# Up products of two FFNs as seven products of 2x2 blocks, weights in pieces, attention transposes moved: a kernel on one Trainium2 core

## The chip, the core and the metric

The kernel runs on one core of a Trainium2 chip. The core's engines work from their own queues: TensorE (PE) multiplies, VectorE (DVE), ScalarE (ACT) and GpSimd (POOL) work on elements, SyncE (SP) issues most of the transfers. The metric is the device time of one execution in microseconds; the figure for a kernel is the median of its runs.

## The reference, cut to what matters

Three blocks are computed on 512 tokens of width 1024, with a context of 256 tokens: two blocks of one kind (attention, pooling and convolution, then an FFN), which the text calls layers 0 and 1, and one of another kind (latent attention and a recurrence, then an FFN), layer 2. All is float32. The change bears on the FFN of layers 1 and 2, where only the 512 tokens are left:

```python
def swiglu(h, w_in, w_out):
    gu = jnp.einsum('bld,de->ble', h, w_in)
    g, u = jnp.split(gu, 2, axis=-1)
    return jnp.einsum('blf,fd->bld', jax.nn.silu(g) * u, w_out)

x = x + g1 * jnp.einsum('blm,md->bld', mix, w_out[l])
x = x + g2 * swiglu(modulate(rms_norm(x, norm2_g[l]), sh2, sc2), w_ffn_in[l], w_ffn_out[l])
```

with 2816 hidden columns. The vectors g1, g2, sh2, sc2 come from a modulation product of a condition vector with a weight w_mod.

## The kernel before, in words

**Products.** A float32 operand is held as two parts, hi (a rounded copy, made by ACT) and lo (the rest, a subtraction on POOL or DVE). `mm3` (L254, L257, L258) makes one product of 128 rows from three matmuls: hi x hi, hi x lo, lo x hi. Activations lie with features on the partitions: `h[k]` is a pair (hh, hl) of 128 features by 512 tokens, k from 0 to 7, and the tokens are worked on in two halves of 256.

**Weights.** The class `Weights` walks a list of all weights in the order of their use, one ahead. A weight of 2048 columns is fetched by SP in two transfers of 512 KB (tiles `raw`, four buffers), and split in four quarters of 512 columns: ACT's cast (L229, `whi`) and POOL's subtraction (L230, `wlo`). The pool `w` has two buffers of 2048 columns for each part.

**The FFN** (`ffn`) runs over 22 slices of 128 hidden columns. For each slice `j` the gate and the up product are each eight `mm3` over k, with 512 tokens as columns (in the first two slices as two times 256, so that the first half's products can run while the second half's norm is made). Then ACT's Silu (L948) and DVE's multiply (L949) read PSUM, ACT and POOL split the result (`gh`, `gl`), and `mod_fill` may put a slot of modulation products (L343) behind it. After a group of slices (the table `DOWN`: 8, 8, 2, 4 in layers 1 and 2) the down products of the group run and DVE adds them into x (`flush`, L888).

**Before the FFN** `out_proj` makes the output projection for one half of the tokens, then for the other; behind each the callback `norms` makes the half's row scale (`row_rms`, whose transposes are L322) and its normalized rows (`norm_apply`: L422, L430 on DVE; L425, L427 on ACT; L428 on POOL).

**Attention** (`attn`, `attn_values`; in layer 2 `mla_values`) goes over heads and blocks of 128 queries: scores of a block, then the values of the block before; with the second block of a pair, right behind its values, DVE's scaling (L862) and PE's two transposes (L865; L1542 in layer 2).

A scheduler puts the instructions of each engine in an order by priorities and estimated costs; each engine then works strictly through its own.

## Time and profile before

| | us |
|---|---|
| median of 3 runs | 2644.15 (2641.61 to 2648.14) |
| the profiled execution | 2645.27 |
| its span | 2643.4 |
| PE busy in it | 2505.2 (95%) |
| POOL, DVE, ACT busy | 1143.5, 959.3, 908.4 |
| mean granted clock of PE | 0.972 |

The profile's span has stages of two kinds: mixing (0 to 420, 1060 to 1400 and 1760 to 2260 us, about) and the FFNs of the layers 0, 1 and 2 between and behind them. PE's shares differ between them, so the share of the whole span says little about one. Durations of DVE and POOL are those between an instruction's start and its end, whatever it waited for inside.

### The profile page before, as it was taken

The numbers are of one execution on the slowest core, as the hardware profiler recorded it, in microseconds if no ns is written. First come the engines' busy times: TensorE is split into PE (matmuls) and PEld (weight loads), VectorE is DVE, ScalarE is ACT, GpSimd is POOL, SyncE is SP. The second block draws the span as 40 slices with busy tenths as digits, with TensorE's granted clock in tenths as the row PEclk, the third lists the DMA queues.
The fourth block names the chain that finished last, engine by engine and source line by source line (L and its number), as shares of the span: only waits on it lengthen the run. The fifth ranks groups of instructions, "written<-read, shape, count | busy, mean of one in ns | idle before, by whom it ended". The sixth has DMA issues, their size and how long they took to land.

```text
span 2643.4 us, 38643 instructions
## 1 busy us (share of the span) xinstructions
PE 2505.2 (95%) x15840; PEld 2134.2 (81%) x15840; DVE 959.3 (36%) x1932; ACT 908.4 (34%) x1905; POOL 1143.5 (43%) x965
## 2 busy tenths in 40 slices
PE   7889979999999999989999999999998899999998
PEld 5778869988888889877788777778887788888887
DVE  4897464221120123488542112113322756210112
ACT  4334443312212123333534223224443543422222
POOL 4544314523333334655326545454322344555553
PEclk9889989999999999999999999999998899999999
DMA  7113311323223222222224434343101021222221
GB/s 252 50 49 112 116 68 33 119 89 112 96 91 103 95 97 99 81 64 81 96 80 144 158 129 160 124 151 106 51 33 50 16 95 50 80 96 96 94 90 57
DMA packets 68961, 248.55 MB, mean 94 GB/s; under 512 B 7472, under 2 KB 10800, under 8 KB 67120
## 3 DMA queue, kind: packets, MB, share of 16 engines
q1 hardware_dynamic: 64992, 231.11, 26.8%
q10 hardware_dynamic: 3792, 14.97, 1.5%
q8 instruction: 125, 2.05, 0.3%
q14 instruction: 52, 0.43, 0.1%
HBM read 239.75 MB, written 6.29 MB: 93 GB/s over the span
## 4 chain that ended last, share of the span: by engine, by line
PE 47%; DVE 6%; ACT 2%; POOL 2%; issue 1%; DMA 1%; POOLq 0%; DVEq 0%; ACTq 0%
PE s2t L254 6%; PE s2t L258 6%; PE s2t L257 6%; PE pj L254 5%; PE pj L257 5%; PE pj L258 5%; PE ap L819 2%; DVE mix L664 1%; PE ap L254 1%; PE ap L257 1%; PE ap L258 1%; POOL wlo L230 1%; PE s2t L1525 1%; PE ap L343 1%; PE s2t L836 1%
## 5 line engine op out<-in xcount | busy, mean ns | idle before, releaser
L230 POOL TENSOR_TENSOR wlo<-raw,whi 128x512 fp32r<-128x512 f32 x576 | 747.2, 1328 | 713.5 <-ACT whi L229 710.3
L229 ACT CAST whi<-raw 128x512 fp32r<-128x512 f32 x576 | 319.7, 616 | 673.3 <-PE pj L257 243.6
L254 PE MATMUL s2t<-hh,whi 128*128 128x512 f32 (+1 forms) x1184 | 448.5, 380 | 1.0 <-ACT whi L229 1.0
L258 PE MATMUL s2t<-hh,wlo 128*128 128x512 f32 (+1 forms) x1184 | 446.7, 377 | 0.0
L257 PE MATMUL s2t<-hl,whi 128*128 128x512 f32 (+1 forms) x1184 | 445.8, 377 | 0.9 <-POOL hl L428 0.9
L254 PE MATMUL pj<-hh,whi 128*128 128x256 f32 (+1 forms) x1088 | 337.6, 312 | 8.0 <-ACT hh L425 2.7
L257 PE MATMUL pj<-hl,whi 128*128 128x256 f32 (+1 forms) x1088 | 332.5, 306 | 3.1 <-POOL hl L428 1.1
L258 PE MATMUL pj<-hh,wlo 128*128 128x256 f32 (+1 forms) x1088 | 331.3, 305 | 0.3 <-POOL wlo L230 0.3
L949 DVE TENSOR_TENSOR sg<-sg,s2t 128x512 f32<-128x512 f32 x66 | 45.4, 687 | 656.5 <-ACT sg L948 656.5
L258 PEld LDWEIGHTS s2t<-hh,wlo 128*128 128x128 f32 x1184 | 222.7, 188 | 46.6 <-issue 1.2
L254 PEld LDWEIGHTS s2t<-hh,whi 128*128 128x128 f32 x1184 | 222.3, 188 | 46.4 <-issue 2.1
L257 PEld LDWEIGHTS s2t<-hl,whi 128*128 128x128 f32 x1184 | 222.5, 188 | 45.8 <-POOL hl L428 1.5
L254 PEld LDWEIGHTS pj<-hh,whi 128*128 128x128 f32 x1088 | 210.6, 194 | 25.5 <-issue 3.7
L327 POOL TENSOR_TENSOR gl<-sg,gh 128x512 fp32r<-128x512 f32 (+1 forms) x66 | 97.5, 1477 | 299.8 <-ACT gh L326 299.8
L257 PEld LDWEIGHTS pj<-hl,whi 128*128 128x128 f32 x1088 | 211.2, 194 | 12.0 <-POOL hl L428 1.4
L258 PEld LDWEIGHTS pj<-hh,wlo 128*128 128x128 f32 x1088 | 210.2, 193 | 8.7 <-POOL wlo L230 0.5
L254 PE MATMUL pj<-whi,hh 128*128 128x256 f32 x672 | 196.8, 293 | 1.3 <-ACT v L699 0.9
L257 PE MATMUL pj<-wlo,hh 128*128 128x256 f32 x672 | 194.6, 290 | 0.0
L258 PE MATMUL pj<-whi,hl 128*128 128x256 f32 x672 | 194.0, 289 | 0.0
L888 DVE SCALAR_TENSOR_TENSOR xt<-pj,mod,xt 128x256 f32<-128x256 f32 x224 | 101.6, 480 | 177.1 <-PE pj L258 176.5
L948 ACT ACTIVATE sg<-s2t 128x512 f32<-128x512 f32 x66 | 39.2, 594 | 314.5 <-PE s2t L258 314.4
L254 PE MATMUL pj<-gh,whi 128*128 128x512 f32 (+1 forms) x400 | 145.6, 367 | 0.0
(382 smaller groups left out, 4581.6 us busy)
## 6 DMA issues: line engine op xcount, KB each, us to landing
raw<-in_w_mod SPq DMA_DIRECT2D x144, 512.0 KB, 3.9
raw<-in_w_up SPq DMA_DIRECT2D x132, 512.0 KB, 3.9
raw<-in_w_dn SPq DMA_DIRECT2D x66, 512.0 KB, 4.0
raw<-in_w_in SPq DMA_DIRECT2D x60, 512.0 KB, 3.9
raw<-in_w_out SPq DMA_DIRECT2D x24, 512.0 KB, 3.8
xt<-xs ACTq DMA_DIRECT2D x4, 1024.0 KB, 5.7
xt<-in_xT ACTq DMA_DIRECT2D x2, 1024.0 KB, 7.8
xs<-xt SPq DMA_DIRECT2D x2, 1024.0 KB, 3.8
```

Of the source, the lines that this page charges most:

```text
L229: nc.scalar.copy(out=h, in_=raw[:, q])
L230: nc.gpsimd.tensor_tensor(out=lo[:, s][:, q], in0=raw[:, q], in1=h.bitcast(F32), op=ALU.subtract)
L254: i = mm(ps, lhsT=lh, rhs=rh, start=start, stop=False)
L257: mm(ps, lhsT=lh, rhs=rl, start=False, stop=False)
L258: return mm(ps, lhsT=ll, rhs=rh, start=False, stop=stop)
L327: (lo_eng or self.nc.vector).tensor_tensor(out=lo, in0=src, in1=hi.bitcast(F32), op=ALU.subtract)
L343: nc.tensor.matmul(ps[g:g + 32], lhsT=self.cond_t[:, k, :], rhs=raw[k // 4][:, k % 4, :], start=k < 4, stop=k >= 4, tile_position=(0, g))
L664: nc.vector.scalar_tensor_tensor(out=m, in0=u[:, j:j + W], scalar=dw(j), in1=m, op0=ALU.mult, op1=ALU.add)
L819: i = nc.tensor.matmul(o, lhsT=at[:, j], rhs=v[:, j0 + j, :], start=j0 + j == 0, stop=j0 + j == nj - 1)
L888: self.nc.vector.scalar_tensor_tensor(out=x, in0=ps, scalar=col, in1=x, op0=ALU.mult, op1=ALU.add)
L948: nc.scalar.activation(out=sg[:, c], in_=p[:, 0], func=AF.Silu)
L949: nc.vector.tensor_tensor(out=sg[:, c], in0=sg[:, c], in1=p[:, 1], op=ALU.mult)
```

## The change

In layers 1 and 2 the gate and up products of one slice are seen as one product of 2x2 blocks: rows are gate (a1x) and up (a2x), the inner dimension is cut into k 0 to 3 and 4 to 7, the tokens into their two halves, b11 to b22. Instead of the eight block products the kernel makes seven, each of 4 k x 3 matmuls with 256 columns, out of sums of blocks: t1 to t4 of the activations (once for each layer) and s1 to s4 of the weights (once for each slice), and seven sums of the results.

- `norms_seven` makes b11 and b21 from the first half of the tokens, and from the second half, for each pair of k, two scaled rows, four differences and five splits (b12 itself is not needed: t1 stands in its place, and t2, t3, b22, t4 follow).
- `_load7` turns a slice's weight into seven pieces of 128x512, in six steps, one behind each product: four sums on DVE (L253, L254, L257, L262), four residues on DVE (L235), three on POOL, seven casts on ACT.
- `up_seven` makes the products, seven sums on DVE from PSUM (L995), and Silu, multiply (L1014, L1017) and split as before.
- All weights lie in pieces of 512 columns (pool `w` has eight buffers for each part), read through `View`.
- `DOWN` of layers 1 and 2 becomes that of layer 0: groups of 4, 4, 4, 4, 2, 4 slices. `MODS_FFN` of layer 1 puts three slots into each of its first two slices, and as many (22) in all.
- `attn_values` and `mla_values` return their transposes as a function `turn`, which the loop calls behind the next scores.

```diff
-DOWN = [
-    [(0, 4, 512), (4, 4, 512), (8, 4, 512), (12, 4, 512), (16, 2, 1024), (18, 4, 512)],
-    [(0, 8, 256), (8, 8, 256), (16, 2, 1024), (18, 4, 512)],
-    [(0, 8, 256), (8, 8, 256), (16, 2, 1024), (18, 4, 512)],
-]
+DOWN = [[(0, 4, 512), (4, 4, 512), (8, 4, 512), (12, 4, 512), (16, 2, 1024), (18, 4, 512)]] * 3
+SEVEN = (1, 2)
...
+    def _split(self, src, lo_eng, pool=None, bufs=None):
+        nc = self.k.nc
+        hi, lo = [(pool or self.k.p_w).tile([128, 512], F32R, tag=t, name=t, bufs=bufs) for t in ("whi", "wlo")]
+        nc.scalar.copy(out=hi, in_=src)
+        lo_eng.tensor_tensor(out=lo, in0=src, in1=hi.bitcast(F32), op=ALU.subtract)
+        return hi, lo
...
+        def first():
+            d["a11"] = self._split(a11, nc.gpsimd)
+            d["t1"], d["t2"] = [k.tmp("sq", [128, 512]) for _ in range(2)]
+            tt(out=d["t1"], in0=a21, in1=a22, op=ALU.add)
+            tt(out=d["t2"], in0=d["t1"], in1=a11, op=ALU.subtract)
+
+        def s3():
+            tt(out=a21, in0=a11, in1=a21, op=ALU.subtract)
+            d["s3"] = self._split(a21, v)
+
+        def s4():
+            d["a12"] = self._split(a12, nc.gpsimd, self.extra, 2)
+            tt(out=a12, in0=a12, in1=d["t2"], op=ALU.subtract)
+            d["s4"] = self._split(a12, v)
...
+        self.todo += [
+            first, lambda: part("s2", lambda: d["t2"], v), s3, lambda: part("s1", lambda: d["t1"], v), s4,
+            lambda: part("a22", lambda: a22, nc.gpsimd, self.extra, 2)]
...
+        p = product(x[:, 0], "a11", "b11")
+        nc.scalar.copy(out=r1, in_=p)
+        p = product(x[:, 1], "s2", "t2")
+        add(u2, r1, p)
+        p = product(y[:, 0], "s3", "t3")
+        add(u3, u2, p)
+        p = product(y[:, 1], "s1", "t1")
+        add(c22, u3, p)
+        add(u2, u2, p)
+        sg = pf.tile([128, 2, 256], F32, tag="sg", name="sg", bufs=2)
+        p = product(self.ps([128, 256]), "s4", "b22")
+        add(u2, u2, p)
+        nc.scalar.activation(out=sg[:, 1], in_=u2, func=AF.Silu)
+        p = product(self.ps([128, 256]), "a12", "b21")
+        add(r1, r1, p)
+        nc.scalar.activation(out=sg[:, 0], in_=r1, func=AF.Silu)
+        nc.vector.tensor_tensor(out=sg[:, 1], in0=sg[:, 1], in1=c22, op=ALU.mult)
+        p = product(self.ps([128, 256]), "a22", "t4")
+        add(u3, u3, p)
+        nc.vector.tensor_tensor(out=sg[:, 0], in0=sg[:, 0], in1=u3, op=ALU.mult)
...
+            for k in range(4):
+                x = value(1, k, r, self.scratch())
+                y = value(1, k + 4, r, self.scratch())
+                p, q = f1[k], f1[k + 4]
+                e, o = (nc.vector, nc.gpsimd)[::1 if k % 2 else -1]
+                sub(nc.vector, p, x, p)
+                self.split(*b["t1"][k], p, e)
+                sub(nc.vector, x, y, x)
+                self.split(*b["b22"][k], y, o)
+                sub(nc.vector, y, y, p)
+                self.split(*b["t2"][k], y, nc.vector)
+                self.split(*b["t3"][k], x, nc.gpsimd)
+                sub(nc.vector, q, q, y)
+                self.split(*b["t4"][k], q, e)
...
-    MODS_FFN = [[1] * NJ, [1] * NJ, [0] * NJ]
+    MODS_FFN = [[1] * NJ, [3, 3] + [1] * 14 + [0] * 2 + [1, 1, 0, 0], [0] * NJ]
...
                     with self.tc.high_priority(300):
                         e, nk = self.attn_scores(pa, l, hd, g, i, qk[hd], og)
-                        if prev is not None:
-                            self.attn_values(*prev)
+                        if turn is not None:
+                            turn()
+                        turn = self.attn_values(*prev) if prev is not None else None
...
-        self.p_w = es.enter_context(tc.tile_pool(name="w", bufs=2))
+        self.p_w = es.enter_context(tc.tile_pool(name="w", bufs=8))
```

Where the instructions come to stand, at three places. In the changed kernel `mm3` is L317, L320, L321; the row scale's transposes are L385; the residue of an activation split is L390.

**First, the start of layer 2's FFN.** On PE before, around the second half's row scale (`rsy`), `s2t` being the tiles of the first half's gate and up products:

```order
L254 MATMUL s2t<-hh,whi 128x256
L257 MATMUL s2t<-hl,whi 128x256
L258 MATMUL s2t<-hh,wlo 128x256
L254 MATMUL s2t<-hh,whi 128x256
L322 MATMUL ap<-ident,rsy 128x128 x2
L257 MATMUL s2t<-hl,whi 128x256
L258 MATMUL s2t<-hh,wlo 128x256
```

On PE after, 13 rows behind the same transposes (`pj` are the products with b21 and b22, `th` and `tl` the two parts of t1 to t4):

```order
L320 MATMUL pj<-hl,whi 128x256
L321 MATMUL pj<-hh,wlo 128x256
L317 MATMUL pj<-hh,whi 128x256
L320 MATMUL pj<-hl,whi 128x256
L321 MATMUL pj<-hh,wlo 128x256
L317 MATMUL s2t<-th,whi 128x256 x2
L320 MATMUL s2t<-tl,whi 128x256
L321 MATMUL s2t<-th,wlo 128x256
L317 MATMUL s2t<-th,whi 128x256
L320 MATMUL s2t<-tl,whi 128x256
L321 MATMUL s2t<-th,wlo 128x256
L317 MATMUL s2t<-th,whi 128x256
```

What moved: before, matmuls with `hh`, `hl` of the first half stand on both sides of the transposes. After, one product (`s2t<-hh`) stands ahead of them and products with b21 and b22 behind them, and the operands `th`, `tl`, of the second half, follow 18 rows on. On DVE before, from the second half's first scaling to the multiplies of the first slices:

```order
L422 SCALAR_TENSOR_TENSOR u<-xt_19628,mod_88,ap 128x256 x4
L430 SCALAR_TENSOR_TENSOR hl<-u,mod_88,hh 128x256
L422 SCALAR_TENSOR_TENSOR u<-xt_19628,mod_88,ap 128x256 x2
L430 SCALAR_TENSOR_TENSOR hl<-u,mod_88,hh 128x256
L422 SCALAR_TENSOR_TENSOR u<-xt_19628,mod_88,ap 128x256 x2
L430 SCALAR_TENSOR_TENSOR hl<-u,mod_88,hh 128x256 x2
L949 TENSOR_TENSOR sg<-sg,s2t 128x512 x8
```

and on DVE after, from the same scaling on:

```order
L1041 SCALAR_TENSOR_TENSOR u<-xt_21828,mod_88,ap 128x256 x4
L235 TENSOR_TENSOR wlo<-sq,whi 128x512
L1054 TENSOR_TENSOR f_22789<-u,f_22789 128x256 x2
L390 TENSOR_TENSOR hl<-u,hh 128x256
L253 TENSOR_TENSOR sq<-raw 128x512
L1054 TENSOR_TENSOR u<-u 128x256 x2
L390 TENSOR_TENSOR hl<-f_22789,hh 128x256
L257 TENSOR_TENSOR raw<-raw 128x512
L1054 TENSOR_TENSOR u<-u,f_22789 128x256 x2
L1054 TENSOR_TENSOR f_22807<-f_22807,u 128x256 x2
L262 TENSOR_TENSOR raw<-raw,sq 128x512
L390 TENSOR_TENSOR tl<-u,th 128x256 x2
```

What moved: the residues of the norm (L430) give way to differences (L1054), residues (L390) and weight steps (L235, L253, L257, L262) in one row; the whole stretch up to the first sum L995 is 30 rows of order.

**Second, a slice in layer 2's FFN.** On DVE a slice before is one row L949 (above, x8 for a group). After, in the first group:

```order
L995 TENSOR_TENSOR nm<-nm,s2t 128x256
L257 TENSOR_TENSOR raw<-raw 128x512
L995 TENSOR_TENSOR rt<-nm,s2t 128x256
L995 TENSOR_TENSOR nm<-nm,pj 128x256
L995 TENSOR_TENSOR rt<-rt,s2t 128x256
L995 TENSOR_TENSOR nm<-nm,s2t 128x256
L262 TENSOR_TENSOR raw<-raw,sq 128x512
L995 TENSOR_TENSOR nm<-nm,pj 128x256
L254 TENSOR_TENSOR sq<-sq,raw 128x512
L235 TENSOR_TENSOR wlo<-raw,whi 128x512
L995 TENSOR_TENSOR rt<-rt,pj 128x256
L1014 TENSOR_TENSOR sg<-sg,rt 128x256
```

What moved: seven sums (L995) and two multiplies stand among the sums and residues of the next slices' weights, in one queue.

**Third, PE in layer 0's attention** at the transposes L865 (L927 after) of the `on` tile that PE waits for at 339.67 us in the trace. Before:

```order
L258 MATMUL pj<-whi,hl 128x256
L791 MATMUL pj<-ident,y 128x128 x4
L819 MATMUL ap<-v,at 128x128 x3
L836 MATMUL s2t<-qk 128x512 x2
L865 MATMUL ap<-ident,on 128x128 x2
```

After:

```order
L896 MATMUL s2t<-qk 128x256 x6
L851 MATMUL pj<-ident,y 128x128 x4
L879 MATMUL ap<-v,at 128x128 x3
L896 MATMUL s2t<-qk 128x512 x2
L927 MATMUL ap<-ident,on 128x128 x2
```

What moved: some transposes and value products around; the row right ahead of the two transposes is the scores' (L836, L896) in both.

## Rows read from the trace of the kernel before

**Rows 1.** The page, busy time, share of the span and instructions of the engines.

```profile
PE 2505.2 (95%) x15840; PEld 2134.2 (81%) x15840; DVE 959.3 (36%) x1932; ACT 908.4 (34%) x1905; POOL 1143.5 (43%) x965
```

**Rows 2.** Table by stretch: length; busy PE, PEld, DVE, ACT, POOL; granted clock; DMA share; GB/s.

```profile
370.00:380.00 10.00, 3.54 (x18) 3.07 (x17) 7.32 (x21) 5.07 (x17) 0.69 (x1) 0.62 0.59 238
1420.00:1760.00 340.00, 340.00 (x1693) 263.38 (x1692) 49.51 (x125) 97.81 (x181) 171.22 (x138) 1.00 0.44 143
2280.00:2600.00 320.00, 320.00 (x1373) 257.45 (x1372) 34.20 (x68) 84.65 (x155) 172.26 (x137) 1.00 0.29 94
```

**Rows 3.** Waits of PE, whole span: us in total, times, longest.

```profile
PE ap L865 <- DVE on L862: 16.0, 5, 6.8
...
PE s L254 <- ACT whi L229: 6.4, 3, 3.2
```

**Rows 4.** Timeline of PE: start, duration, instruction, idle time before it and releaser.

```profile
339.67 0.66 PE L865 MATMUL ap<-ident,on 128*128 128x128 f32 x2 [6.81 <-DVE on L862]
...
377.00 0.66 PE L865 MATMUL ap<-ident,on 128*128 128x128 f32 x2 [6.46 <-DVE on L862]
...
1399.99 0.29 PE L254 MATMUL s2t<-hh,whi 128*128 128x256 f32 x1
1400.11 0.28 PE L257 MATMUL s2t<-hl,whi 128*128 128x256 f32 x1
```

**Rows 5.** Timeline of DVE, the same columns.

```profile
371.58 3.77 DVE L327 TENSOR_TENSOR hl<-mix,hh 128x256 fp32r<-128x256 f32 x11
...
1398.17 1.66 DVE L422 SCALAR_TENSOR_TENSOR u<-xt,mod,ap 128x256 f32<-128x256 f32 x4 [1.79 <-PE ap L322]
...
1424.65 0.69 DVE L949 TENSOR_TENSOR sg<-sg,s2t 128x512 f32<-128x512 f32 x1 [1.46 <-ACT sg L948]
...
1447.04 0.69 DVE L949 TENSOR_TENSOR sg<-sg,s2t 128x512 f32<-128x512 f32 x1 [11.32 <-ACT sg L948]
...
1459.61 0.69 DVE L949 TENSOR_TENSOR sg<-sg,s2t 128x512 f32<-128x512 f32 x1 [11.51 <-ACT sg L948]
...
2255.89 0.48 DVE L430 SCALAR_TENSOR_TENSOR hl<-u,mod,hh 128x256 fp32r<-128x256 f32 x1
...
2260.83 1.66 DVE L422 SCALAR_TENSOR_TENSOR u<-xt,mod,ap 128x256 f32<-128x256 f32 x4 [2.40 <-PE ap L322]
...
2266.53 0.48 DVE L430 SCALAR_TENSOR_TENSOR hl<-u,mod,hh 128x256 fp32r<-128x256 f32 x1 [0.19 <-ACT hh L425]
...
2280.78 0.69 DVE L949 TENSOR_TENSOR sg<-sg,s2t 128x512 f32<-128x512 f32 x1 [3.54 <-ACT sg L948]
...
2304.15 0.69 DVE L949 TENSOR_TENSOR sg<-sg,s2t 128x512 f32<-128x512 f32 x1 [10.51 <-ACT sg L948]
2315.35 0.69 DVE L949 TENSOR_TENSOR sg<-sg,s2t 128x512 f32<-128x512 f32 x1 [10.51 <-ACT sg L948]
```

**Rows 6.** Instructions by line, PE, 1396 to 1424.5 us: count, busy us, mean ns.

```profile
L343 PE MATMUL ap<-raw,cond 128*32 128x256 f32 x32 | 3.0, 388 | 0.0
```

**Rows 7.** The same view, DVE, whole span, forms apart.

```profile
L430 DVE SCALAR_TENSOR_TENSOR hl<-u,mod,hh 128x256 fp32r<-128x256 f32 x52 | 38.0, 736 | 8.0 <-ACT hh L425 7.8
...
L779 DVE TENSOR_TENSOR sq<-nm,sg 128x256 f32<-128x256 f32 x32 | 29.6, 967 | 0.3
...
L949 DVE TENSOR_TENSOR sg<-sg,pj 128x256 f32<-128x256 f32 x22 | 9.3, 422 | 129.7 <-ACT sg L948 129.7
...
L327 DVE TENSOR_TENSOR hl<-om,hh 128x512 fp32r<-128x512 f32 x4 | 3.7, 928 | 0.0
...
L327 DVE TENSOR_TENSOR hl<-oml,hh 128x512 fp32r<-128x512 f32 x4 | 2.7, 684 | 0.0
```

**Rows 8.** The same view, POOL, whole span.

```profile
L230 POOL TENSOR_TENSOR wlo<-raw,whi 128x512 fp32r<-128x512 f32 x572 | 744.1, 1332 | 713.5 <-ACT whi L229 710.3 <-PE pj L258 2.8
L327 POOL TENSOR_TENSOR gl<-sg,gh 128x512 fp32r<-128x512 f32 x44 | 57.1, 1297 | 77.2 <-ACT gh L326 77.2
...
L428 POOL TENSOR_TENSOR hl<-u,hh 128x256 fp32r<-128x256 f32 x52 | 39.5, 765 | 32.5 <-ACT u L427 32.5
```

More of the change, by code (lines that the diff above doesn't have):

```diff
@@ L220, in _load @@
             return raws
-        p = k.p_w
-        hi = p.tile([128, n], F32R, tag="whi", name="whi")
-        lo = p.tile([128, n], F32R, tag="wlo", name="wlo")
+        if kind == "seven":
+            return self._load7(ap)
+        pieces = []
         for s in halves:
@@ L226, in _load @@
             nc.sync.dma_start(out=raw, in_=ap[:, s])
-            for q in (slice(0, hn // 2), slice(hn // 2, hn)):
-                h = hi[:, s][:, q]
-                nc.scalar.copy(out=h, in_=raw[:, q])
-                nc.gpsimd.tensor_tensor(out=lo[:, s][:, q], in0=raw[:, q], in1=h.bitcast(F32), op=ALU.subtract)
-        return hi, lo
+            for q in range(0, hn, 512):
+                pieces.append(self._split(raw[:, q:q + 512], nc.gpsimd))
+        return pieces
     def next(self, key):
+        self.step(len(self.todo))
         while self.done < min(len(self.specs), self.used + 1 + self.ahead):
@@ L914, in out_proj, with up_seven, product @@
                 after(i if xc is not None else i + 1)
+    def up_seven(self, l, j, pf, b, gt):
+        nc = self.nc
+        w = self.W.next(("up", l, j))
+        x, y = [self.s2([128, 2, NX])[:, :, 0:256] for _ in range(2)]
+        def product(ps, a, t):
+            for k in range(4):
+                cs = slice(k * 128, k * 128 + 128)
+                self.mm3(ps, w[a][0][:, cs], w[a][1][:, cs], *b[t][k], k == 0, k == 3)
+            self.W.step()
+            return ps
+        add = lambda out, x, y: nc.vector.tensor_tensor(out=out, in0=x, in1=y, op=ALU.add)
+        ru, uc = self.tmp("nm", [128, 2, 256]), self.tmp("rt", [128, 2, 256])
+        r1, u2, u3, c22 = ru[:, 0], ru[:, 1], uc[:, 0], uc[:, 1]
+        p = product(x[:, 0], "a11", "b11")
[18 more added lines that the diff above has]
+        nc.vector.tensor_tensor(out=sg[:, 0], in0=sg[:, 0], in1=u3, op=ALU.mult)
+        gh = pf.tile([128, NX], F32R, tag="gh", name="gh")
+        gl = pf.tile([128, NX], F32R, tag="gl", name="gl")
+        self.split(gh, gl, sg.rearrange("p a b -> p (a b)"), nc.gpsimd)
+        gt.append((gh, gl))
@@ new lines, in seven @@
+    def seven(self, pf, h):
+        pair = lambda: tuple(pf.tile([128, 256], F32R, tag="t" + p, name="t" + p, bufs=12) for p in "hl")
+        cut = lambda ks, c: [(h[k][0][:, c], h[k][1][:, c]) for k in ks]
+        self.W.extra = pf
+        a, c = slice(0, 256), slice(256, 512)
+        b = {"b11": cut(range(4), a), "t1": cut(range(4), c), "b21": cut(range(4, 8), a), "b22": cut(range(4, 8), c)}
+        b.update({t: [pair() for _ in range(4)] for t in ("t2", "t3", "t4")})
+        return b
@@ L1674, in ffn @@
                 for j in range(j0, j0 + jn):
-                    std(("up", l, j), I[f"w_up{l}"][j])
+                    specs.append((("up", l, j), "seven" if l in SEVEN else "w", I[f"w_up{l}"][j], 2048))
                 for s in range(D // cn):
```

143 lines of the change are left out of this document (100 added, 43 removed).

## Prediction, made before the changed kernel ran

> **What bounds the kernel now.** I read the page's busy shares first, then the table by stage, then what the matmul engine waits for, and last the durations of single instructions. TensorE (PE) is busy for 95% of the span [rows 1]. By stage the picture is sharper: in the second and third FFN it is busy without a gap, 340.00 us of 340.00 and 320.00 of 320.00, at full clock, while VectorE (DVE) works 49.51 and 34.20 us there and GpSimd (POOL) 171.22 and 172.26 [rows 2]. So in these two stages the end is set by the number of matmuls and nothing else; a matmul less is time less, until another engine comes near. That is where the change acts, with 22 slices of hidden columns in each of the two layers. Its attention part aims at something else: PE's waits at the transposes of L865, 16.0 us in five waits [rows 3].
>
> **Matmuls saved.** The third FFN's slices come every 2315.35 - 2304.15 = 11.20 us [rows 5]; a slice is 48 matmuls of 512 columns, so one takes 0.233 us. In the second FFN one modulation slot is added to a slice, 1459.61 - 1447.04 = 12.57 us [rows 5], so a slot costs 1.37. After, a slice is 7 products x 4 x 3 = 84 matmuls of 256 columns. These start 0.12 us apart, each with its own weight load hidden [rows 4]; with 0.119, half of 0.233 and 2% more, a slice takes 10.0 us. 1.19 us saved x 44 slices = **-52.4 us**, the most that the products can give. The price is work elsewhere: per slice DVE goes from one instruction to 17, ScalarE from four weight casts to seven; POOL goes from four weight residues to three.
>
> **Start of the two FFNs.** This is the largest cost. Now the second half of the norm runs under the first half's products: in the third FFN DVE begins it at 2260.83, its last residue starts at 2266.53, PE has no gap behind it, and the multiply (L949) of the second slice starts at 2280.78; in the second FFN the norm's second half starts at 1398.17 and that multiply at 1424.65 [rows 5]. After, every operand but the first half's two needs the second half of the tokens, and DVE has this to do between the second half's row scale and the first product sum: 8 scalings at 1.66 us for four [rows 5], 3.3 us; 16 differences and 10 residues of 128x256 at 3.77/11 = 0.343 us when run back to back [rows 5], 8.9 us; and the order puts some six weight steps of 128x512 among them, 0.60 each (0.684 in the mean [rows 7], less the 0.08 that running back to back takes off a 128x256 of 0.422), 3.6 us. That is 15.8 us undisturbed. How much POOL disturbs them is the unknown. A DVE instruction with two operands in SBUF can take longer than its shortest: L430 takes 0.48 in a single row [rows 5] and 0.736 in the mean, the 128x512 residue 0.684 in one stage and 0.928 in another, L779 even 0.967 where L949's 128x256, with an operand in PSUM, takes 0.422 [rows 7]. So the extra per instruction lies between 0 and 0.55. I take 0.18, a little under the two middle rows (0.24 and 0.26), since POOL has work for some 60% of this stretch (13 us, below). 32 x 0.18 = 5.8, so 21.6 us (15.8 to 33). Then ten products of 12 x 0.119 = 1.43 us, 14.3 in all, still stand in PE's order up to the second slice's last one; one of them belongs to the third slice. The second slice's products then end at 2260.83 + 21.6 + 12.9 = 2295.3; now they end some 0.6 us before L949, at 2280.2, and with two cheaper slices it would be 2277.8: **+17.5 us** (11 to 29). For the second FFN 1398.17 + 21.6 + 12.9 = 1432.7 against 1421.6, +11; but the change puts six modulation slots into the first two slices, into this wait, where 32 matmuls (four slots of eight) ran beside the norm before [rows 6], and the later slices lose four slots of 1.37, of which I count 4 us: **+7 us** (1 to 19). PE gets only about five products, 7 us, into each wait, in pieces between four pairs of operands. In the ten us around a wait of 6.46 us the granted clock was 0.62 in the mean [rows 2], half speed (1.2 GHz of 2.4) for most of them; ten us of work at that clock lose 3.8. I put 2.5 for each start, **+5 us** (0 to 8).
>
> **Slices in the steady state.** Per slice DVE has eight steps of 128x512 (four sums, four residues), 8 x 0.60 = 4.8, and seven sums and two multiplies of 128x256, 9 x 0.343 = 3.1: 7.9 us, and with 0.2 on the ten that read two operands from SBUF 9.9. (With every instruction alone, 0.684 and 0.422, and 0.24 on ten, it is 11.7.) In the second FFN the period is 11.4 with its slot, in the third 10.0. So DVE, which had 34 us of work in 320, comes just under PE. The down products (22 us for each four slices, 96 x 0.233) let it catch up, and the order keeps weights about a slice ahead, and two or three products (2.9 to 4.3 us) between a product and the reuse of its PSUM tile. What remains is slip inside a group of four: I take 0.45 us for each of the third FFN's slices and nothing for the second's, **+10 us** (0 to 35). POOL has per slice 3 x 1.332 + 1.297 = 5.3 us [rows 8], no bound by itself.
>
> **The rest.** Weights in pieces of 512 columns let a product begin when its first piece is there. PE's wait for them is the row of 6.4 us [rows 3]; I count **-3** (-8 to 0). The attention transposes stand behind the next scores in the code, but at the two great waits (6.81 and 6.46 us [rows 4]) the scheduler already had scores and other work in front; at the first the row in front of the transposes is the same as before, at the second only one product of values has come in front of them, and DVE still has the residues of the pooling branch, 3.77 us in one run [rows 5], ahead of the scaling that PE waits for. **-2** (-10 to +2). Groups of four for down add two groups to each of the two layers, 16 flushes each, which hang on PE's own products: **+1** (0 to 4).
>
> **Sum.** -52.4 + 17.5 + 7 + 5 + 10 - 3 - 2 + 1 = -16.9. The profiled execution took 2645.3 us (span 2643.4 and 1.9 around it), 1.1 above the median of the runs, so 2628.4 against the profile and about **2628 us** against the runs.
>
> **Rival 1: the starts are covered.** If PE can work through the first half's operands of several slices while DVE transforms, and DVE keeps ahead, a third of the 39.5 us of starts, clock and slip remains: -52.4 + 13 - 4 = -43.4, about 2601. For it: two of the seven operands need only the first half. Against it: PE goes in order, and the order has five products there.
>
> **Rival 2: DVE bounds the third FFN's slices.** Its ten two-operand instructions need 0.33 us extra each, in place of 0.2, to bring 7.9 to 11.2 us; then the third FFN gains nothing per slice, 22 x 1.19 = 26 where I have 10, and 2628 + 16 = 2644 us, no change. For it: 0.24, 0.26 and 0.55 are in the rows [rows 7]. Against it: the down products give 5.6 us per slice on average, if the buffers reach so far.
>
> **Rival 3, the other side: DVE and POOL exclude each other.** Then what counts is the sum of POOL's instructions and DVE's with two SBUF operands. Per slice 5.3 + 8 x 0.60 to 0.684 + 2 x 0.343 to 0.422 = 10.8 to 11.6 us: nothing gained per slice in the third FFN, as in rival 2. In the starts POOL's ten splits (0.765 [rows 8]) and some four weight residues (1.332), 13 us, stand in line with DVE's 12.5 us of two-operand work and 3.3 of scalings: 28.8 us in place of 21.6, 7 more in each. 2644 + 14 = 2658 us, slower than before. It decides from where 4 us of POOL's 13 in each start are no longer beside DVE's work: 2644 + 2 x 4 = 2652. For it: the means far above the shortest, L779 at 0.967 [rows 7]. Against it: a DVE instruction that meets a POOL one would wait for half of its 1.332 us on average, 0.67, and the two middle rows show 0.24 and 0.26 more.
>
> The Trainium skill states this rival as a rule (SBUF — State Buffer, section "SBUF: two separate sides"): VectorE with two SBUF inputs and a GpSimd instruction that reads SBUF share a port pair by an exclusive lock, and the later one waits for the whole of the other instruction. By that rule the time is rival 3's, above 2650; by the means of the rows it is the forecast's. The rows agree that instructions with two SBUF operands stretch; they don't show that each of them waits out a whole one.
>
> **How the numbers follow.** Forecast (partial gain, 2612 to 2642) 0.45; rival 1 0.12; rival 2 0.23; rival 3 0.20. A measurement of this kernel can tell about 0.3%, 8 us: faster is below 2636, slower above 2652. Faster: 0.85 of the forecast's share, rival 1, a sixth of rival 2: 0.54. Slower: rival 3 but a tenth of it, and a tenth of rival 2: 0.20. No change: the rest, 0.26. The range takes in rival 1 at its lower end and rival 3 at its upper: 2600 to 2662; below it would need both starts covered and the attention waits gone, above it rival 3 with slip in the second FFN too.
>
> **What would show it.** In the profile after: 256-column matmuls 0.119 apart and slices 10.0 us apart in the third FFN (more shows the slip, and PE's waits should then name DVE's or ScalarE's weight steps); between the second half's row scale and the first sum of L995 about 22 us in the third FFN, with PE waiting for th or tl; DVE's L235 near 0.8 us in the mean; PE's waits at the transposes still near 14 us. If L235 takes 0.9 us or more, or POOL's wlo 1.6, rival 3 holds. The forecast is wrong if PE waits for weights in the second FFN, whose period I take as free, or if the starts cost under 10 or over 35 us together.

## The result: 1.1% slower

The changed kernel takes 2677.3 us in the median (2673.0 to 2682.9, four runs) against 2642.9 for the kernel before (2641.6 to 2648.1, four runs): a ratio of 1.0114, with an interval of 1.0091 to 1.0137 (the medians themselves stand 1.3% apart). It is slower by 30 to 34 us, above the range of the prediction and beyond the time of its rival 3. The profiled execution after took 2682.9 us, 5.6 above its median; the tables by stage below go by profiled executions.

The page of the kernel after, busy time and share of each engine (answers to [rows 1]):

```profile
PE 2503.9 (93%) x17232; PEld 2195.8 (82%) x17232; DVE 1425.9 (53%) x2744; ACT 1026.3 (38%) x2163; POOL 1136.8 (42%) x931
...
DVE  4887564112021205485565667763324657777775
```

TensorE is busy about as long as before, though the products should have taken 52 us off it, and VectorE has gained 467 us. The second line is VectorE's in 40 slices: in the second FFN (digits 22 to 27) and the third (35 to 39) it works at 0.5 to 0.7, where it stood at 0.15 and 0.11 in the stretches of [rows 2].

The table by stretch, columns as in [rows 2]: the second FFN's slices, the third FFN's, and the start of the third, in a wider and a narrower window:

```profile
1437.00:1785.00 348.00, 339.55 (x2440) 298.68 (x2438) 240.09 (x466) 144.21 (x286) 166.81 (x126) 1.00 0.42 141
2312.00:2646.00 334.00, 313.07 (x2097) 286.36 (x2096) 246.69 (x410) 129.21 (x252) 171.44 (x121) 0.97 0.28 91
2262.00:2312.00 50.00, 38.36 (x241) 34.59 (x240) 42.89 (x83) 30.08 (x72) 26.73 (x22) 0.80 0.10 32
2269.00:2301.00 32.00, 21.77 (x107) 18.63 (x106) 26.75 (x52) 17.70 (x41) 18.46 (x16) 0.68 0.07 25
```

Where TensorE was busy for every microsecond, it now idles 8 of 348 us in the second FFN's slices, 21 of 334 in the third's and 10 of 32 in the third's start, and the granted clock is 0.97 in the third's slices and 0.68 in its start. DVE is busy for 74% of the slices of the third FFN, and in the start it and POOL together are busy for 26.75 + 18.46 us in 32, so for 13 us at least they work at the same time.

Where the difference arose, worked out from the traces. Stages are cut at transposes of row scales: at 471.2, 1053.6, 1800.5, 2260.3 and 2625.6 us before, at the same instructions at 454.2, 1038.1, 1803.9, 2269.5 and 2663.3 us after. The cut between second mixing and second FFN shifts with the order of the matmuls, so these stand as one. The row "forecast" puts the terms of the prediction into the same stages.

| us | 1st mixing | 1st FFN | 2nd mixing + FFN | 3rd mixing | 3rd FFN | tail |
|---|---|---|---|---|---|---|
| before | 471.2 | 582.3 | 746.9 | 459.9 | 365.2 | 17.9 |
| after | 454.2 | 583.9 | 765.7 | 465.6 | 393.7 | 17.9 |
| difference | -17.0 | +1.6 | +18.8 | +5.7 | +28.5 | 0 |
| forecast | -5.0 | 0 | -16.2 | 0 | +4.3 | 0 |

The miss is 54.5 us between profiled executions: 35.0 in the second mixing stage and FFN, 24.2 in the third FFN, 7.3 elsewhere, less 12.0 that the first mixing stage gained unforeseen.

The whole third FFN before, after, and with three causes away (an experiment below), columns as in [rows 2]:

```profile
2260.30:2625.60 365.30, 363.53 (x1713) 299.54 (x1712) 47.01 (x95) 103.02 (x192) 191.24 (x156) 1.00 0.26 84
```

```profile
2269.50:2663.30 393.80, 362.73 (x2433) 333.02 (x2434) 288.19 (x488) 157.39 (x316) 200.28 (x146) 0.95 0.24 80
```

```profile
2259.60:2600.30 340.70, 339.06 (x2414) 318.21 (x2413) 221.60 (x454) 198.70 (x393) 35.23 (x28) 1.00 0.27 92
```

PE idles 31.1 us of the stage after, 1.8 before. A granted clock of 0.95 over 394 us is some 20 us more (an estimate). Idle time and clock together are most of the 28.5 + 26.2 us that this stage lost against what the products should have given.

**The new waits.** What PE waits for in the third FFN's slices, 2312 to 2646 us (columns as in [rows 3]), and below it DVE's waits there up to 2640 us:

```profile
PE pj L317 <- DVE rt L995: 11.7, 4, 3.2
PE s2t L317 <- DVE nm L995: 3.8, 3, 2.3
PE pj L321 <- DVE wlo L235: 1.8, 4, 1.2
```

```profile
DVE raw L262 <- POOL wlo L235: 15.7, 9, 2.5
DVE sq L253 <- DMA raw<-in_w_up: 12.7, 8, 3.1
DVE wlo L235 <- ACT whi L234: 11.1, 9, 1.7
```

The largest wait is for a product sum, four times: at the ends of the first four groups of slices. One of them on DVE (start, duration, instruction, idle time before it and releaser), on POOL, and on PE:

```profile
2397.34 1.12 DVE L1014 TENSOR_TENSOR sg<-sg,rt 128x256 f32<-128x256 f32 x1 [0.87 <-ACT sg L1010]
2400.47 0.95 DVE L253 TENSOR_TENSOR sq<-raw 128x512 f32<-128x512 f32 x1 [2.01 <-DMA raw<-in_w_up]
2401.45 1.65 DVE L254 TENSOR_TENSOR sq<-sq,raw 128x512 f32<-128x512 f32 x1
2403.02 1.74 DVE L257 TENSOR_TENSOR raw<-raw 128x512 f32<-128x512 f32 x1
2404.69 0.41 DVE L995 TENSOR_TENSOR rt<-rt,pj 128x256 f32<-128x256 f32 x1
2405.13 1.05 DVE L1017 TENSOR_TENSOR sg<-sg,rt 128x256 f32<-128x256 f32 x1
```

```profile
2399.58 6.32 POOL L235 TENSOR_TENSOR wlo<-raw,whi 128x512 fp32r<-128x512 f32 x4
```

```profile
2405.16 0.57 PE L317 MATMUL pj<-gh,whi 128*128 128x512 f32 x1 [3.12 <-DVE rt L995]
2405.53 0.63 PE L320 MATMUL pj<-gl,whi 128*128 128x512 f32 x1
2405.95 0.63 PE L321 MATMUL pj<-gh,wlo 128*128 128x512 f32 x1
```

Two things meet here. DVE's queue goes in order, and in it the first three weight sums of the next group's first slice (L253, L254, L257) stand ahead of the last product sum of this group (L995). They begin with a wait for a transfer, 2.01 us. Then they take 0.95, 1.65 and 1.74 us, where a 128x512 instruction can take 0.684, beside POOL's four residues of 6.32 us. PE has the down products behind them, which need the PSUM tile `pj` that L995 frees: it stands for 3.12 us, and its next matmuls come 0.42 apart where 512 columns took 0.233. That is the lower level of the clock, as the stretch shows in which they run (columns as in [rows 2]):

```profile
2406.00:2408.00 2.00, 2.00 (x6) 1.60 (x5) 0.78 (x2) 1.66 (x3) 1.09 (x1) 0.50 0.00 0
```

The instruction of 0.41 in the middle, whose one operand is in PSUM, is not stretched at all.

DVE's instructions with two operands in SBUF over the whole span, forms apart (columns as in [rows 6]), and one PSUM form behind them:

```profile
L235 DVE TENSOR_TENSOR wlo<-sq,whi 128x512 fp32r<-128x512 f32 x88 | 76.1, 865 | 10.8 <-ACT whi L234 9.6 <-PE pj L320 1.0
...
L257 DVE TENSOR_TENSOR raw<-raw 128x512 f32<-128x512 f32 x44 | 46.0, 1044 | 0.3
L254 DVE TENSOR_TENSOR sq<-sq,raw 128x512 f32<-128x512 f32 x44 | 43.0, 977 | 0.5
...
L1017 DVE TENSOR_TENSOR sg<-sg,rt 128x256 f32<-128x256 f32 x44 | 37.2, 845 | 0.6
...
L995 DVE TENSOR_TENSOR nm<-nm,pj 128x256 f32<-128x256 f32 x88 | 36.4, 415 | 23.3 <-PE pj L321 22.7
```

and POOL's weight residues, in the same view [rows 8] of the kernel after:

```profile
L235 POOL TENSOR_TENSOR wlo<-raw,whi 128x512 fp32r<-128x512 f32 x530 | 723.4, 1388 | 725.3 <-ACT whi L234 536.3 <-PE pj L320 160.2 <-PE ap L406 10.8
```

A mean hides how the extra comes. Of DVE's instructions with two SBUF operands in the third FFN's slices (2312 to 2646 us, 189 of them), 100 ran while POOL had no elementwise instruction, and none of these took more than 0.1 us above its shortest. The other 89 overlapped one: 70 of them were stretched by more than 0.1 us, by 0.77 in the mean, and the mean of all 89 is 0.61.

### The profile page after: what moved, and what is told of

Its sections match the earlier page's. It is cut to its first block, busy times and chain, and to the rows that moved or that the text cites. A ratio compares the mean times of both kernels' runs of the same rounds, so it can differ in the third digit from the quotient of the medians.

```text
span 2681.1 us, 43150 instructions
## 1 busy us (share of the span) xinstructions
PE 2503.9 (93%) x17232; PEld 2195.8 (82%) x17232; DVE 1425.9 (53%) x2744; ACT 1026.3 (38%) x2163; POOL 1136.8 (42%) x931
## 5 line engine op out<-in xcount | busy, mean ns | idle before, releaser
L235 POOL TENSOR_TENSOR wlo<-raw,whi 128x512 fp32r<-128x512 f32 x530 | 723.4, 1388 | 725.3 <-ACT whi L234 536.3
L317 PE MATMUL pj<-hh,whi 128*128 128x256 f32 (+1 forms) x1440 | 440.8, 308 | 10.4 <-ACT hh L389 3.0
L320 PE MATMUL pj<-hl,whi 128*128 128x256 f32 (+1 forms) x1440 | 434.7, 302 | 9.8 <-DVE hl L390 3.6
L321 PE MATMUL pj<-hh,wlo 128*128 128x256 f32 (+1 forms) x1440 | 434.0, 302 | 1.8 <-DVE wlo L235 1.8
L317 PEld LDWEIGHTS pj<-hh,whi 128*128 128x128 f32 x1440 | 279.2, 194 | 31.6 <-issue 5.1
L320 PEld LDWEIGHTS pj<-hl,whi 128*128 128x128 f32 x1440 | 279.7, 194 | 22.6 <-DVE hl L390 4.7
L321 PEld LDWEIGHTS pj<-hh,wlo 128*128 128x128 f32 x1440 | 278.7, 194 | 11.9 <-DVE wlo L235 2.6
L317 PE MATMUL s2t<-hh,whi 128*128 128x256 f32 (+1 forms) x768 | 259.4, 339 | 10.8 <-DVE nm L995 4.2
L320 PE MATMUL s2t<-hl,whi 128*128 128x256 f32 (+1 forms) x768 | 258.8, 337 | 0.9 <-DVE hl L390 0.8
L321 PE MATMUL s2t<-hh,wlo 128*128 128x256 f32 (+1 forms) x768 | 258.8, 337 | 0.8 <-POOL wlo L235 0.8
L390 POOL TENSOR_TENSOR gl<-sg,gh 128x512 fp32r<-128x512 f32 (+1 forms) x66 | 101.2, 1534 | 289.0 <-ACT gh L389 289.0
L317 PE MATMUL pj<-whi,hh 128*128 128x256 f32 x672 | 196.7, 293 | 1.7 <-ACT ev L412 0.9
L321 PE MATMUL pj<-whi,hl 128*128 128x256 f32 x672 | 195.4, 291 | 0.0
L320 PE MATMUL pj<-wlo,hh 128*128 128x256 f32 x672 | 195.1, 290 | 0.0
L317 PEld LDWEIGHTS s2t<-hh,whi 128*128 128x128 f32 x768 | 145.6, 190 | 33.1 <-ACT whi L234 6.3
L320 PEld LDWEIGHTS s2t<-hl,whi 128*128 128x128 f32 x768 | 146.2, 190 | 19.2 <-DVE hl L390 1.2
L321 PEld LDWEIGHTS s2t<-hh,wlo 128*128 128x128 f32 x768 | 145.9, 190 | 16.9 <-POOL wlo L235 1.5
L317 PE MATMUL pj<-gh,whi 128*128 128x512 f32 (+1 forms) x400 | 147.9, 372 | 11.7 <-DVE rt L995 11.7
L321 PE MATMUL pj<-gh,wlo 128*128 128x512 f32 (+1 forms) x400 | 148.4, 371 | 0.0
L320 PE MATMUL pj<-gl,whi 128*128 128x512 f32 (+1 forms) x400 | 147.4, 369 | 0.0
```

What stands on the lines that cost most here:

```text
L235: lo_eng.tensor_tensor(out=lo, in0=src, in1=hi.bitcast(F32), op=ALU.subtract)
L317: i = mm(ps, lhsT=lh, rhs=rh, start=start, stop=False)
L320: mm(ps, lhsT=lh, rhs=rl, start=False, stop=False)
L321: return mm(ps, lhsT=ll, rhs=rh, start=False, stop=stop)
L390: (lo_eng or self.nc.vector).tensor_tensor(out=lo, in0=src, in1=hi.bitcast(F32), op=ALU.subtract)
```

## The experiments

The theory after this reading: in the two FFNs DVE's and POOL's work on SBUF goes in turns (rival 3), and the order of DVE's queue turns that into waits of PE at the group ends; the starts come on top. The rivals: DVE has simply too much work (rival 2); the starts alone cost it all; the loss comes from the other parts of the change. Ratios are against the kernel before on the same chip; differences in us are those of the medians. By the ratios those to the changed kernel come out some 4 to 6 us smaller.

**Without the seven products** (pieces and attention order kept), and the same with groups of four:

```diff
...
-SEVEN = (1, 2)
+SEVEN = ()
...
```

> The seven products, their norms, the groups of four for down and the modulation table of the second layer are undone; weights in pieces and the moved attention transposes stay. In the trace of the changed kernel the first mixing stage and its FFN start 16 us earlier, the second mixing stage gives 14 back and the third loses another 7 to 9. If these shifts come from the pieces and the transposes alone, this run ends 5 to 8 us above the kernel before, near 2650 us, and its mixing stages show the same shifts. If pieces and transposes are worth the 5 us that the prediction counted, it ends near 2638, and the losses in the second and third mixing stage belong to the seven products (to the order they force on the queues around them).

> The kernel of e1 with the changed kernel's groups of four for the down products in the second and third layer. The prediction counted +1 us for the groups (0 to 4). With 48 matmuls of 512 columns a slice and one VectorE instruction, nothing else stands in the way at a group's end: within 4 us of e1, 2625 to 2631. If a group's end costs by itself (the last slice's split is on the way to the down products), four more ends in two layers cost 2 to 3 us each: 2635 and more.

Measured 2626.7 us, ratio 0.9939 (0.9924 to 0.9954), and with groups of four 2628.0, 0.9934 (0.9919 to 0.9949). Of the two times expected for the first, 2650 and 2638, neither came: the other parts gain 16 us. The groups of four make no difference clear of the noise (1.3 us more in the medians, the other way by the ratios); the seven products alone cost 2677.3 - 2628.0 = 49 us. These two are the best versions with nothing left out, and faster than both kernels.

**Pieces alone** (each attention transpose again right behind its values):

```diff
...
-                        if turn is not None:
-                            turn()
-                        turn = self.attn_values(*prev) if prev is not None else None
+                        if prev is not None:
+                            turn = self.attn_values(*prev)
+                            if turn is not None:
+                                turn()
...
```

> The kernel of e1 with the attention transposes back behind their own values: of the change only the weights in pieces of 512 columns are left. e1 ended 16 us below the kernel before. If the moved transposes bring these 16 us (its first mixing stage is 16 us shorter, and there the transposes waited), this run ends near 2641. If the pieces bring them (a product begins when its first piece is there, and the scheduler's order moves), it stays near 2627. The prediction counted -3 for the pieces and -2 for the transposes.

Measured 2630.5, 0.9958 (0.9943 to 0.9973). Of the gain of 16 us the pieces bring about 12. The other 4 would be the transposes', but the intervals of the two kernels overlap. By stages the first mixing stage takes 471.2 before, 459.0 with pieces, 454.1 with both; the other kernels that have both take from 452.2 to 458.1 there, so this stage does not show a gain of the transposes either.

**Weight sums held back.** The first sum of a group's first slice goes behind the last multiply of the group before:

```diff
...
-            tt(out=d["t1"], in0=a21, in1=a22, op=ALU.add)
+            i = tt(out=d["t1"], in0=a21, in1=a22, op=ALU.add)
+            if hold and k.last is not None:
+                k.order(i, k.last)
...
```

> The changed kernel with one more order on VectorE: the first weight sum of a group's first slice stands behind the last multiply of the group before. Theory A (a queue's order): at four group ends of the third FFN the last product's sum stands behind three weight sums, the first of which waits for its transfer; PE then waits 3.3 us and runs at half clock for 1.5 more. Then these four waits vanish, the third FFN becomes 15 to 20 us shorter and the kernel ends at 2657 to 2662 us. Theory B (VectorE and GpSimd simply have too much to do): the work moves behind the multiply and is missed by the next group's first products; the third FFN keeps its length within 5 us, the kernel stays at 2672 to 2680.

Measured 2662.9, 1.0079 (1.0064 to 1.0094), 14 us less than the changed kernel. PE's greatest waits in its third FFN are

```profile
PE ap L323 <- POOL gl L393: 4.8, 3, 1.6
PE s2t L320 <- DVE nm L998: 2.1, 2, 1.6
```

so the four waits for `rt`, 11.7 us, are gone (lines are 3 higher here), and 4.8 us stand in their place for POOL's residue of the gate. The third FFN takes 383.7 in place of 393.7. That is 10 us where 15 to 20 were expected from the queue's order, but not nothing, as it would be if DVE's load alone counted.

**POOL's part of the two layers' weights away.** Three residues of a slice's weights and those of down become plain copies on ScalarE; DVE's work is unchanged:

```diff
...
+        if lo_eng is self.k.nc.scalar:
+            lo_eng.copy(out=lo, in_=src)
...
-            d["a11"] = self._split(a11, nc.gpsimd)
+            d["a11"] = self._split(a11, nc.scalar)
...
```

> In the FFN of the second and third layer the weight residues that GpSimd makes are replaced by a plain copy on ScalarE, so that GpSimd has only the split of the products left; the residues are then wrong in value, the work on TensorE and VectorE is the same. Theory B (VectorE's two-operand instructions are stretched by GpSimd, rival 3 of the prediction): the weight sums and residues fall from 0.74 to 1.04 us to about 0.69, and of the 53 us that the steady slices and the 20 and more that the starts lost, 25 us or more come back: below 2652. Theory A: the stretch matters only at the group ends, where three sums would take 2.0 in place of 4.3 us: 4 x 2.3, about 9 us, and the kernel ends near 2667. ScalarE takes some 0.62 us more for each of the 4.5 residues of a slice, which brings it to about 9 of 10 us; if it becomes the bound, PE waits for its casts and the time rises above 2677.

Measured 2633.0, 0.9962 (0.995 to 0.9973): 44 us less than the changed kernel. The same lines of DVE as above, in its trace (3 higher here too):

```profile
L257 DVE TENSOR_TENSOR sq<-sq,raw 128x512 f32<-128x512 f32 x44 | 31.9, 724 | 0.8
...
L260 DVE TENSOR_TENSOR raw<-raw 128x512 f32<-128x512 f32 x44 | 30.1, 684 | 0.2
L1020 DVE TENSOR_TENSOR sg<-sg,rt 128x256 f32<-128x256 f32 x44 | 19.0, 432 | 1.6
```

The sums fall from 0.977 and 1.044 to 0.724 and 0.684 us, the multiply from 0.845 to 0.432, with not one instruction of DVE's taken away. This speaks against rival 2: the number of DVE's instructions is not what costs. The gain of the third FFN, 27.4 us, lies in its slices and not in its start: from the second slice's last multiply to the end of the stage it takes 324.8 us in place of 352.1.

**The third FFN without the second half's transform** (its operands are those of the first half under other names):

```diff
...
+        if l == 2:
+            b.update({"t1": b["b11"], "t2": b["b21"], "t3": b["b11"], "t4": b["b21"], "b22": b["b11"]})
...
```

> In the third layer's FFN the operands t1 to t4 and b22 are replaced by the first half's two, so the second half's scaled rows, their differences and splits are left out (the row scale stays); products, weights and sums of results are all there. This takes the whole price of the third FFN's start away: in the trace of the changed kernel the second slice ends 43 us behind the row scale's transposes where the kernel before needs 21, so if the transform is that price, 20 to 24 us come back: about 2655 us. If the start is held by the weights' first pieces or by something else, less than 8 us come back.

Measured 2659.8, 1.0069 (1.0047 to 1.009): 17.5 us less, all of it in the third FFN (376.2 in place of 393.7), where 20 to 24 were expected. The waits for `rt` are still there, 14.8 us in four.

**POOL's residues moved to DVE**, nothing left out; three weight residues, those of a11, a12 and a22, and that of the gate, 3 x 1.388 + 1.383 = 5.5 us of POOL's work per slice:

```diff
...
-            d["a11"] = self._split(a11, nc.gpsimd)
+            d["a11"] = self._split(a11, v)
...
-        self.split(gh, gl, sg.rearrange("p a b -> p (a b)"), nc.gpsimd)
+        self.split(gh, gl, sg.rearrange("p a b -> p (a b)"), nc.vector)
...
```

> The changed kernel with the three weight residues of a slice and the residue of its result moved from GpSimd to VectorE (nothing is left out); GpSimd keeps the down weights' residues. If the two engines exclude each other for instructions with two SBUF operands, what counts is the sum of both: a residue holds 1.39 us on GpSimd and 0.69 on VectorE, so per slice 4 x 0.7 = 2.8 us of the sum go away, VectorE has 7.9 + 4 x 0.6 = 10.3 us per slice nearly undisturbed, and the kernel gains 10 us or more: below 2667. If VectorE's own load is what binds, 2.4 us more per slice make the up phases of the third FFN slower than 10.3 us a slice and the kernel ends above 2680.

Measured 2646.1, 1.0011 (0.9997 to 1.0024). DVE has four instructions more per slice, and the kernel is 31 us faster than the changed one. This is the test that tells rivals 2 and 3 apart: by rival 2 it should have been slower. In the slices POOL keeps only the residues of down's weights, in runs, so its trace shows both cases side by side. POOL, then DVE around the end of such a run:

```profile
2369.01 11.31 POOL L235 TENSOR_TENSOR wlo<-raw,whi 128x512 fp32r<-128x512 f32 x8 [52.12 <-ACT whi L234]
```

```profile
2371.03 0.82 DVE L1017 TENSOR_TENSOR sg<-sg,rt 128x256 f32<-128x256 f32 x1
2371.77 1.51 DVE L1014 TENSOR_TENSOR sg<-sg,rt 128x256 f32<-128x256 f32 x1
2373.39 0.42 DVE L995 TENSOR_TENSOR rt<-nm,s2t 128x256 f32<-128x256 f32 x1
...
2379.43 1.44 DVE L235 TENSOR_TENSOR wlo<-raw,whi 128x512 fp32r<-128x512 f32 x1
2380.79 0.68 DVE L254 TENSOR_TENSOR sq<-sq,raw 128x512 f32<-128x512 f32 x1
2381.40 0.68 DVE L257 TENSOR_TENSOR raw<-raw 128x512 f32<-128x512 f32 x1
2382.00 0.41 DVE L1014 TENSOR_TENSOR sg<-sg,rt 128x256 f32<-128x256 f32 x1
```

POOL's run ends at 2380.32. Until then a multiply of two SBUF operands takes 0.82 and 1.51 us, a residue 1.44; from then on each takes its shortest, 0.41 and 0.68. L995 with its operand in PSUM takes 0.42 inside the run.

One thing this run and the one with POOL's part away don't part. In the changed kernel DVE also waits for POOL's results: L262 overwrites the piece whose residue POOL still has to make, 15.7 us in nine waits in the third FFN (above). With the residues moved to DVE these waits go too, and with copies on ScalarE 6.7 us are left. What the two give back is the price of POOL's work beside DVE's as a whole; that the stretching is the larger part is an estimate, 89 x 0.61 = 54 us of DVE's time in the same slices against 15.7.

**Both cures**, nothing left out: the sums held back and POOL's residues on DVE.

> The changed kernel, nothing left out, with the order of e2 and the residues of e5. Singly they gave 14 and 31 us. If GpSimd's stretch was what made the group ends late, e5 has most of e2 already: 2640 to 2646. If they are separate, 2630 to 2635. For a kernel with the seven products to pay, it must come below e1's 2627; I expect it does not.

Measured 2644.6, 1.0003 (0.9992 to 1.0014). The hold, worth 14 us by itself, adds nothing that can be measured: with POOL's work moved, the sums ahead of the last product sum are short, and the largest wait for `rt` is one of 0.9 us. So with the residues on DVE the order of the queue costs nothing: it did cost beside the stretching.

**Three causes away** (sums held, POOL's part away, third FFN's transform away), then also the second FFN's transform (its down results are then multiplied by zero), then also four buffers of their own for the modulation weights of the second FFN:

```diff
...
-                raw = k.p_raw.tile([128, hn], F32, tag="raw", name="raw")
+                raw = (k.p_mod or k.p_raw).tile([128, hn], F32, tag="mraw" if k.p_mod else "raw", name="raw", bufs=4 if k.p_mod else None)
...
```

> The changes of e2, e3 and e4 together: the added order at the group ends, GpSimd's weight residues in the FFN of the second and third layer as copies on ScalarE (wrong in value), the second half's transform of the third FFN left out. Singly they gave 14, 44 and 17.5 us. If these are separate causes they add up to 76: near 2601 us, and with e1's 2627 - 52 = 2575 as the kernel in which the products cost nothing beside themselves, 26 would stay open (the second FFN's start among it). If the group ends and the starts are mostly late because of GpSimd, they are one cause: e3's 2633 less 10 to 15, 2618 to 2623.

> The kernel of e7 with the second half's transform left out in the second FFN too (its operands are the first half's two; its down results are multiplied by zero before they reach x, so that the numbers stay finite). e7's second FFN took 401 us where the kernel without the seven products (e1) takes 392, although 26 us of products and 5 of slots were to be saved. If the second FFN's start costs what the prediction counted (7 to 9 us) or what the trace of the changed kernel shows (the second slice ends 42 us behind the row scale's transposes, 27 before), 10 to 15 us go: near 2603. If something in the steady slices of the second FFN binds (the four raw buffers, which modulation weights and seven-piece weights share), less than 6 go: above 2610.

> The kernel of e8 with four more raw buffers in the second FFN that take the modulation weights up to its slice 19 (there is room, since the transform's operands are gone). If the shared raw buffers hold the second FFN's slices back (VectorE waits there 33.6 us for transfers of up weights in the changed kernel, where the trace of before has no such wait on the path), 10 us or more go against e8. If transfers are only waited for and not missed, the two end within 4 us.

Measured 2616.0 (0.9898, 0.9874 to 0.9922), 2601.8 (0.984, 0.9818 to 0.9862) and 2596.5 (0.9819, 0.9797 to 0.9841). By stages:

| us | 2nd mixing + FFN | 3rd FFN |
|---|---|---|
| after | 765.7 | 393.7 |
| sums held | 759.9 | 383.7 |
| POOL's part away | 748.1 | 366.3 |
| third FFN's transform away | 766.2 | 376.2 |
| residues on DVE | 759.9 | 363.3 |
| three causes away | 753.1 | 340.7 |
| and second FFN's transform | 737.1 | 341.3 |
| and own modulation buffers | 735.6 | 340.8 |
| without the seven products | 747.2 | 364.4 |

In the third FFN the three causes, taken away one at a time, give 10.0 + 27.4 + 17.5 = 54.9 us, together 53.0. They nearly add up, but are not independent: behind the second slice the hold gives 11.0 us alone, but hold and missing transform together only 5.7 on top of POOL's part, and the missing transform alone gives 20.9 ahead of that point and loses 3.3 behind it. What is left, 340.7, is 2.5 above 364.4 less the 26.2 of the products, so that stage is accounted for. Over the whole kernel the three don't add up: 76 us singly, 61 together. The difference is mostly in the second FFN. There 746.9 - 26.2 = 720.7 was to be had and 765.7 came, 45 us lost: POOL's part alone gives back 17.6, the sums held 5.8, but both together only 12.6; the start costs 16.0, the shared buffers 1.5 (not clear of the noise), and 15 us stay open (10 by the run with POOL's part alone away). What I did not try there: more weight buffers in the full kernel. The third mixing stage lies between 451.6 and 466.5 us in all kernels, without a pattern that I could put down to an edit, so its +5.7 stays open too.

## Why the prediction was wrong

**Products, -52.4: the size was right in the third FFN, as a gross figure.** With its three causes away, it is 23.7 us shorter than with the old products (364.4 to 340.7), 26.2 forecast. In the second no run shows it: the last version has 747.2 - 735.6 = 11.6.

**Start of the third FFN, +17.5: right.** From DVE's second row scale to its first product sum, 2269.98 to 2292.95:

```profile
2269.98 1.66 DVE L1041 SCALAR_TENSOR_TENSOR u<-xt,mod,ap 128x256 f32<-128x256 f32 x4 [0.74 <-PE ap L385]
...
2292.95 0.42 DVE L995 TENSOR_TENSOR nm<-nm,s2t 128x256 f32<-128x256 f32 x1 [0.55 <-PE s2t L321]
```

23.0 us, for 21.6 forecast. The parts were not quite those of the sum: DVE also waits 1.9 us for residues of POOL's there and 0.55 for PE, which the sum did not have, and its stretching, some 4.7 us, is a little under the 5.8 of the forecast. The transform away gives back 17.5 in its stage, which includes what the clock lost there, for which I had 2.5 more. **Start of the second, +7 and 2.5 for the clock: too small**, 16.0 in its stage and 14 in the medians. The modulation slots moved into this wait did not cover what I credited them with; my own range went to 19.

**Steady slices, +10: the step that failed.** It had two parts. For the third FFN I took 0.45 us of slip per slice, 10 us. Behind its second slice this stage takes 352.1 us, and 319.1 with the three causes away: 33 us, 1.5 per slice. POOL's part away gives back 27.3 of it by itself, the queue's order 11.0 by itself. For the second I took nothing, since its period has a slot more; there POOL's part and order cost 13 to 18, and another 10 to 15 is not explained.

In the sum, the term that was too small is the stretching, and the step behind it is how I used a mean. I took 0.2 us for each of ten instructions. Over both FFNs the ten lie 0.23 above their shortest, but in the third FFN's slices 0.29, which by the same sum is 7.9 + 2.9 = 10.8 us for a period of 10.0. And I took a sum just under the period, 9.9, to be hidden. But the extra does not come as a mean: L1014 takes from 0.41 to 1.51 us where L995, with an operand in PSUM, hardly varies (shortest, median and longest in ns):

```profile
L1014 DVE TENSOR_TENSOR sg<-sg,rt x44: 410/424/1511, 1426.1 to 2644.3; 128x256 f32<-128x256 f32 x44
```

```profile
L995 DVE TENSOR_TENSOR nm<-nm,pj x88: 404/415/422, 1419.5 to 2643.4; 128x256 f32<-128x256 f32 x88
```

An instruction meets POOL and loses up to 1.1, or meets none and loses nothing, and it comes in clusters, wherever POOL has a run of residues. DVE also has waits in its queue that the sum did not count, for POOL's residues, for transfers and for ScalarE's casts, 15.7, 12.7 and 11.1 us in the third FFN. I had set the down products against all slip, and the group ends, where they begin, are exactly where PE stood.

**Rival 3 had the right mechanism**, with 0.20 of the chance, and at 2658 was still 19 us too low: it counted the second FFN's slices as free and did not have the group ends. What I held against it was a misreading: an instruction that meets POOL should lose 0.67 us, and two rows show 0.24 and 0.26. Those rows are means over instructions that met POOL and others that did not (the 0.928 is of four that took 0.68, 0.68, 0.83 and 1.52); those that met it lose 0.61 in the changed kernel. The sign by which I meant to know it was wrong too: L235 at 0.9 us or POOL's at 1.6. They came out at 0.865 and 1.388, under both bounds, while the sums stood at 0.98 and 1.04 and the multiply at twice its shortest. POOL's instruction was hardly longer than before, 1.332 [rows 8]: most of the price fell on DVE's side. A mean of one line was the wrong gauge; the spread of an instruction, beside one of the same shape with a PSUM operand, is the right one. [rows 7] has the hint in its means (0.967 against 0.422), and the trace of before has the spread:

```profile
L779 DVE TENSOR_TENSOR sq<-nm,sg x32: 400/1108/1519, 110.7 to 1302.7; 128x256 f32<-128x256 f32 x32
```

The Trainium skill's rule (SBUF — State Buffer, section "SBUF: two separate sides"), that a VectorE instruction with two SBUF inputs and a GpSimd one that reads SBUF lock each other out, the second until the first is done, agrees with this: stretched inside POOL's run, shortest behind it, and no effect with an operand in PSUM. The longest extra is 1.1 us beside POOL's 1.39 to 1.58, and 0.61 in the mean of those that met POOL, about what waiting for the rest of an instruction under way would give (an estimate, half of 1.39).

**The rest.** Pieces were forecast at -3 and gave about -12, outside my range of -8; only PE's wait that named weights was counted, while the whole first mixing stage became 12 us shorter; which of its products carry that I have not taken apart. The transposes were forecast at -2 and gave at most some -4, not clear of the noise, PE's wait at them going from 16.0 [rows 3] to

```profile
PE ap L927 <- DVE on L922: 13.3, 4, 5.8
```

where 14 had been forecast. Groups of four: +1 forecast, nothing clear of the noise measured.

## What to carry to other kernels

Here fewer matmuls paid only where the engines that make and mend their operands stayed clear of each other. So add up GpSimd's work on SBUF and VectorE's with two SBUF operands as one load, and where that sum nears the period, give the work to the engine that does it in less time (four residues a slice moved from GpSimd's 1.39 us to VectorE's 0.7 gained 31 us although VectorE was the busier, and with that the kernel drew level with the one before). Then look at what stands, in an in-order queue, ahead of the last instruction that frees a tile for TensorE: a prefetch that waits for a transfer does not belong there. And measure the parts of a change apart: here weights in pieces and a later transpose gave 16 us, and the part with the great promise cost three times as much.

## What the runs showed of the hardware

A VectorE instruction of two SBUF operands that meets a GpSimd run took up to 1.1 us more at both sizes: 0.41 became 1.51 for 128x256, and 0.68 became 1.79 for 128x512, at most. I had expected a few tenths for each, spread evenly. And after each wait of 2.3 to 3.2 us at a group end TensorE's next six to eight matmuls came at about half the pace (0.42 us for 512 columns in place of 0.233, at a granted clock of 0.50), some 1.6 us more for each wait: here short waits that recur cost half as much again as their length.
